# A fused two-layer transformer kernel: Strassen chunks with tiles of their own, a later start in their group, and y taken four tiles at a time

## The chip, the cores and the metric

One core of a Trainium2 chip runs the whole model in one launch. The metric is the device time of one execution in microseconds. The kernel before was run three times: 2220.4, 2224.18 and 2230.65 us, median 2224.18 us.

## What is computed

Two layers on 256 tokens of width 2048 in float32: stick-breaking attention with an MLP, then a sparse attention with three branches and an MLP. The change is in the two MLPs (layer 0 and layer 1):

```python
D_MODEL, SEQ, D_FF = 2048, 256, 4 * 2048

def sqrelu_mlp(h, w1, w2):
    return jnp.square(jax.nn.relu(h @ w1)) @ w2

for layer in range(2):
    h = h + (stick_breaking_attention, native_sparse_attention)[layer](rms_norm(h, ...), ...)
    h = h + sqrelu_mlp(rms_norm(h, mlp_norm_g[layer]), mlp_w1[layer], mlp_w2[layer])
```

## The kernel before, in words

**Products.** A float32 matrix is split in two parts, a rounded one (hi) and the rest (lo); of a product, hi times hi, lo times hi and hi times lo are summed in PSUM. The activations are split once. The weights come from HBM in chunks of 128x1024 float32 (512 KB, two slices of 128 rows by 512 columns), one DMA each on SP's queue (`load`, L130). For each chunk ScalarE (ACT) writes hi (L125), VectorE (DVE) writes lo as the difference (L127), then TensorE (PE) reads both. The raw chunks have five slots (`wraw`), the hi parts four (`whi`), the lo parts four (`wlo`). So a load can be issued only when the chunk five loads before it has been read to the end, which is when DVE has written its lo part.

**An MLP** (`mlp`, L418) goes through four groups `fg` of 2048 hidden columns. `group1` makes y = relu(x w1)^2 for the group: four blocks `fb` of four PSUM banks, eight chunks each (`proj_T2`, L186). After each block, two tiles of 128x256 at a time, ACT and DVE take y out of PSUM (L433 to L454): adds, relu and row factor, square, split in yhi and ylo, and four sums `q` that are split into `ss` for the Strassen block.

`group2` multiplies y with w2: four output blocks `nb` of 512 columns, eight chunks (k) each. Blocks 0, 1 and 3 are plain: `chunk_N` (L143), 12 matmuls of 512 columns. Block 2 takes one level of a Strassen-like scheme: `chunk_S` (L234) does seven half-size products in place of eight, 21 matmuls of 256 columns, and needs sums of the weight quarters. For such a chunk DVE makes four sums `ts` (L243, L247, L248), ACT writes the hi part of the plain quarters (L246, 768 columns) and of the sums (L125), DVE the lo part of the sums (L127) and of the plain quarters (L250). Both pairs come from the same four hi and four lo slots. PE takes first the 14 products with hi weights, then the 7 with lo weights.

**Order of the work.** `order` in `group2` (L459 to L465) lists the chunks as PE takes them and as SP loads them. Below, N0 to N23 are the plain chunks in that order (block 0, then 1, then 3) and S0 to S7 the Strassen ones. In the first three groups of a layer it is N0 N1 S0 N2 N3 S1 and so on to S7, then N16 to N23; in the last group S0 S1 N0 N1 S2 N2 N3 N4 N5 S3 and on by two. The order on DVE and ACT is set by a scheduler when the program is built; each of these engines then takes its instructions strictly as listed.

Of the kernel before, what the change touches and what calls it, by code (L numbers as in the profile page):

```python
# [8 lines left out]
F32 = mybir.dt.float32  # L9
# [30 lines left out]
def hybrid_kernel(  # L40
# [193 lines left out]
    def chunk_S(ps, src, k0, n0, first, last, ahi, alo, shi, slo, koff=0):  # L234


        W = NB // 2
        raw = load(src, k0, KC, n0, NB)
        flat = raw.rearrange("p k n -> p (k n)")

        ts = wsum.tile([P, 4, W], F32, tag="ts", name="ts")
        b12 = flat[:, 3 * W:].unsqueeze(1).to_broadcast([P, 2, W])
        nc.vector.tensor_tensor(ts[:, :2, :], flat[:, W:3 * W].rearrange("p (a n) -> p a n", a=2), b12, op=OP.subtract)  # L243
        hi = whi.tile([P, KC, NB], F32R, tag="hi", name="hi").rearrange("p k n -> p (k n)")
        lo = wlo.tile([P, KC, NB], F32R, tag="lo", name="lo").rearrange("p k n -> p (k n)")
        nc.scalar.activation(hi[:, :3 * W], flat[:, :3 * W], AF.Copy)  # L246
        nc.vector.tensor_tensor(ts[:, 2, :], ts[:, 0, :], flat[:, 2 * W:3 * W], op=OP.add)  # L247
        nc.vector.tensor_tensor(ts[:, 3, :], flat[:, :W], ts[:, 2, :], op=OP.subtract)  # L248
        thi, tlo = split(ts)
        nc.vector.tensor_tensor(lo[:, :3 * W], flat[:, :3 * W], hi[:, :3 * W].bitcast(F32), op=OP.subtract)  # L250
        k = k0 - koff
        y = lambda a, kk, t: a[:, k + kk, t * P:(t + 1) * P]
        s = lambda a, i: a[:, k // KC, i, :]
        b = lambda w, i: w[:, i * W:(i + 1) * W]
        trivial = [
            (0, y(ahi, 1, 0), y(alo, 1, 0), b(hi, 2), b(lo, 2)),
            (1, y(ahi, 0, 0), y(alo, 0, 0), b(hi, 0), b(lo, 0)),
            (2, s(shi, 3), s(slo, 3), b(hi, 1), b(lo, 1)),
        ]
        sums = [  # L260
            (6, s(shi, 2), s(slo, 2), thi[:, 0, :], tlo[:, 0, :]),
            (4, s(shi, 0), s(slo, 0), thi[:, 1, :], tlo[:, 1, :]),
            (5, s(shi, 1), s(slo, 1), thi[:, 2, :], tlo[:, 2, :]),
            (3, y(ahi, 0, 1), y(alo, 0, 1), thi[:, 3, :], tlo[:, 3, :]),
        ]

        def mm(i, a, w, s, e):
            nc.tensor.matmul(ps[i], a, w, start=s, stop=e, skip_group_check=True)  # L268

        for i, xh, xl, wh, wl in trivial + sums:  # L270

# [14 lines left out]
    def add_S(nb, bs, ps, pool):  # L286

        W = NB // 2
        u = pool.tile([P, 2, W], F32, tag="part", name="u")
        v = pool.tile([P, 2, W], F32, tag="pre", name="v")  # L290
        hb = [h[:, t, nb * NB:(nb + 1) * NB] for t in range(NT)]
        nc.scalar.activation(u[:, 0, :], ps[0], AF.Copy)
        nc.vector.tensor_tensor(v[:, 0, :], ps[5], u[:, 0, :], op=OP.add)
# [29 lines left out]
            )  # L323


    def make_x(kp, g0):

        ps = bank(att, "att")
        for j in range(2):
            for t in range(NT):  # L330
                nc.tensor.transpose(  # L331
# [24 lines left out]
    def next_x(layer, nb, g0):  # L356

        ssq(layer, nb, D // NB)
        for kp in range(nb * (NB // P), (nb + 1) * (NB // P), 2):
            yield  # L360
            make_x(kp, g0)

    def rsqrt(v, n):
        r = small.tile([P, 8], F32, tag="rsq", name="rsq", bufs=4)
# [53 lines left out]
    def mlp(l, layer, junk, done, last=None):  # L418
# [9 lines left out]
        def group1(fg, pools):  # L428

            for fb in range(D // NB):  # L430
                ps = [bank(*pools[fb % 2]) for _ in range(NB // P)]
                proj_T2(ps, w1, fg * D + fb * NB)
                for b in range(2):  # L433
                    k = fb * (NB // P) + 2 * b
                    c = junk.tile([P, 2, T], F32, tag="part", name="part")
                    a = junk.tile([P, 2, T], F32, tag="pre", name="pre")
                    for j in range(2):
                        nc.scalar.activation(c[:, j, :], ps[2 * b + j][:, T:], AF.Copy)
                        nc.vector.tensor_tensor(a[:, j, :], ps[2 * b + j][:, :T], c[:, j, :], op=OP.add)
                    nc.vector.scalar_tensor_tensor(  # L440
                        a, a, 0.0, row.unsqueeze(1).to_broadcast([P, 2, T]), op0=OP.max, op1=OP.mult
                    )
                    s = junk.tile([P, 2, T], F32, tag="sq", name="sq")
                    nc.scalar.activation(s, a, AF.Square)
                    nc.scalar.activation(yhi[:, k:k + 2, :], s, AF.Copy)
                    nc.vector.tensor_tensor(ylo[:, k:k + 2, :], s, yhi[:, k:k + 2, :].bitcast(F32), op=OP.subtract)

                    a1, a2 = [[s[:, kk, t * P:(t + 1) * P] for kk in (1, 0)] for t in range(NT)]
                    q = junk.tile([P, 4, P], F32, tag="sums", name="sums")
                    nc.vector.scalar_tensor_tensor(q[:, 0, :], a2[0], -1.0, a2[1], op0=OP.mult, op1=OP.subtract)  # L450
                    nc.vector.tensor_tensor(q[:, 2, :], a1[0], a2[0], op=OP.subtract)
                    nc.vector.tensor_tensor(q[:, 1, :], a2[1], q[:, 2, :], op=OP.subtract)
                    nc.vector.tensor_tensor(q[:, 3, :], a1[1], q[:, 1, :], op=OP.subtract)
                    split_evac(ss[:, 0, k // 2], ss[:, 1, k // 2], q)  # L454

        def group2(fg, plain, strassen, end):

            NK = KD // KC
            order = []  # L459
            for i in range(NK):  # L460
                pq = [(j // NK, j % NK) for j in (2 * i, 2 * i + 1)]
                order += [(2, i)] + pq if end else pq + [(2, i)]
            if end:
                order.insert(1, order.pop(3))
            order += [(3, i) for i in range(NK)]  # L465
            for nb, i in order:
                k0 = fg * KD + i * KC
                args = (w2, k0, nb * NB, i == 0, i == NK - 1, yhi, ylo)
                if nb == 2:
# [14 lines left out]
                if i == NK - 1:
# [2 lines left out]
                        return  # L487
                    add_h(nb, ps)
                    if end and nb == 3:
                        done(nb)  # L490
# [206 lines left out]

    with tc.tile_pool(name="m0p", bufs=2) as mp:
        wsum = mp
        def done0(nb):  # L700
            spawn(next_x("nsa", nb, G_NSA), 1.5)

        mlp(0, "m0", mp, done0)

# [352 lines left out]
    with tc.tile_pool(name="m1p", bufs=2) as mp:  # L1057
        wsum = mp
        ov = out[0].rearrange("(t p) d -> p t d", p=P)

        def done1(nb):
# [33 lines left out]
```

## Time and profile before

| what | value |
|---|---|
| median of three runs | 2224.18 us |
| the profiled execution | 2223.57 us, span 2221.8 us |
| PE busy, share of the span | 99% |
| DVE busy | 1542.2 us, 69% |
| ACT busy | 1226.2 us, 55% |
| mean granted TensorE clock | 0.998 |
| HBM traffic | 182 GB/s over the span |

Engines: PE is the matmul engine, PEld its weight loads, DVE VectorE, ACT ScalarE, SP the queue that issues the loads. Matmuls are pipelined: the duration shown for one is longer than the distance to the next, so a busy PE share of 99% does not exclude waits; they show in the length of a stretch.

### The profile page before, as it was taken

The page shows a single profiled execution, that of the slowest core. Times are in us where ns is not written, and L with a number is a line of the kernel's source. Part 1 is how long each engine was busy: PE and PEld are TensorE (multiplying, and loading weights), DVE is VectorE, ACT ScalarE, POOL GpSimd, SP SyncE. Part 2 cuts the span into 40 slices and gives each one's busy share as a digit, 9 for nine tenths or more (in the row PEclk, how much of TensorE's full clock was granted, in tenths as well). Part 3 has the DMA queues.
Part 4 walks back from the last instruction along what each step waited for, and adds up shares of the span by engine and source line. Part 5 has one row for each costly group of instructions (what it writes and reads, how often), then busy time and mean ns, then how long its engine had stood idle before and what let it go on. Part 6 is the DMA issues. An engine that isn't in the chain of part 4 may idle for free.

```text
span 2221.8 us, 31529 instructions
## 1 busy us (share of the span) xinstructions
PE 2197.6 (99%) x11922; PEld 1880.5 (85%) x11922; DVE 1542.2 (69%) x2320; ACT 1226.2 (55%) x1793; POOL 43.4 (2%) x75
## 2 busy tenths in 40 slices
PE   9999999999999999999999999999999999999999
PEld 9888888888888888888887888888888888888887
DVE  4656655677677677668777777756876776776785
ACT  5555665564455465455555666655644544554553
POOL 0000000000000000000000011000000000000000
PEclk9999999999999999999999999999999999999999
DMA  6655555656665665665667544456566557656655
GB/s 225 205 169 171 166 170 179 187 170 189 211 189 168 213 190 171 208 190 170 211 185 215 158 145 141 135 164 187 172 197 202 171 173 224 182 169 210 190 172 169
DMA packets 260769, 405.99 MB, mean 183 GB/s; under 512 B 13188, under 2 KB 91912, under 8 KB 260616
## 3 DMA queue, kind: packets, MB, share of 16 engines
q1 hardware_dynamic: 259800, 403.52, 58.2%
q8 instruction: 93, 1.52, 0.3%
q14 instruction: 60, 0.49, 0.1%
q10 hardware_dynamic: 816, 0.46, 0.1%
HBM read 401.83 MB, written 2.10 MB: 182 GB/s over the span
## 4 chain that ended last, share of the span: by engine, by line
PE 91%; DMA 4%; DVE 4%; issue 1%; ACT 0%; POOL 0%; DVEq 0%; ACTq 0%; SPq 0%; POOLq 0%
PE acc L147 33%; PE acc L193 11%; PE att L193 11%; PE att L147 6%; PE acc L213 5%; PE att L199 5%; PE acc L199 5%; DMA raw<-in_mlp_w_dram 4%; PE att L268 4%; PE acc L219 3%; DVE lo L127 2%; PE acc L176 2%; PE acc L268 1%; DVE lo L250 1%; PE att L331 1%
## 5 line engine op out<-in xcount | busy, mean ns | idle before, releaser
L125 ACT ACTIVATE hi<-raw 128x1024 fp32r<-128x1024 f32 x687 | 726.5, 1060 | 717.9 <-PE acc L147 268.0
L127 DVE TENSOR_TENSOR lo<-raw,hi 128x1024 fp32r<-128x1024 f32 x687 | 834.7, 1223 | 401.1 <-ACT hi L125 379.8
L147 PE MATMUL acc<-hi,yhi 128*128 128x512 f32 x828 | 327.0, 395 | 0.0
L147 PE MATMUL acc<-hi,ylo 128*128 128x512 f32 x828 | 325.0, 393 | 0.0
L193 PE MATMUL acc<-xs,hi 128*128 128x512 f32 x1024 | 259.8, 396 | 0.0
L193 PE MATMUL att<-xs,hi 128*128 128x512 f32 x1024 | 259.1, 395 | 0.0
L147 PE MATMUL acc<-lo,yhi 128*128 128x512 f32 x828 | 225.3, 393 | 1.1 <-DVE lo L127 1.1
L193 PEld LDWEIGHTS acc<-xs,hi 128*128 128x128 f32 x1024 | 183.0, 188 | 34.7 <-DVE h L387 0.3
L193 PEld LDWEIGHTS att<-xs,hi 128*128 128x128 f32 x1024 | 183.2, 188 | 34.5
L147 PEld LDWEIGHTS acc<-lo,yhi 128*128 128x128 f32 x828 | 154.8, 188 | 35.6 <-DVE lo L127 1.9
L147 PEld LDWEIGHTS acc<-hi,yhi 128*128 128x128 f32 x828 | 155.9, 188 | 31.7 <-ACT yhi L317 0.2
L147 PEld LDWEIGHTS acc<-hi,ylo 128*128 128x128 f32 x828 | 156.0, 188 | 31.3 <-DVE ylo L318 0.2
L147 PE MATMUL acc<-hi,xs 128*128 128x512 f32 x704 | 178.4, 394 | 0.0
L147 PEld LDWEIGHTS acc<-hi,xs 128*128 128x128 f32 x704 | 130.4, 188 | 27.4
L199 PEld LDWEIGHTS acc<-xs,lo 128*128 128x128 f32 x1024 | 135.9, 188 | 11.6
L199 PEld LDWEIGHTS att<-xs,lo 128*128 128x128 f32 x1024 | 135.9, 188 | 11.6
L199 PE MATMUL acc<-xs,lo 128*128 128x256 f32 x1024 | 137.6, 277 | 0.0
L199 PE MATMUL att<-xs,lo 128*128 128x256 f32 x1024 | 137.5, 277 | 0.0
L213 PE MATMUL acc<-xs,hi 128*128 128x512 f32 x512 | 130.3, 396 | 0.0
L243 DVE TENSOR_TENSOR ts<-raw 128x512 f32<-128x512 f32 x64 | 44.2, 691 | 103.8 <-DMA raw<-in_mlp_w_dram 103.8
L213 PEld LDWEIGHTS acc<-xs,hi 128*128 128x128 f32 x512 | 91.8, 188 | 17.5
L125 ACT ACTIVATE hi<-ts 128x1024 fp32r<-128x1024 f32 x64 | 67.6, 1056 | 65.1 <-DVE ts L248 46.7
(281 smaller groups left out, 2862.1 us busy)
## 6 DMA issues: line engine op xcount, KB each, us to landing
raw<-in_mlp_w_dram SPq DMA_DIRECT2D x512, 512.0 KB, 3.9
raw<-in_sb_w_qkv_dram SPq DMA_DIRECT2D x95, 512.0 KB, 3.9
raw<-in_nsa_w_in_dram SPq DMA_DIRECT2D x50, 512.0 KB, 3.6
raw<-in_sb_w_out_dram SPq DMA_DIRECT2D x32, 512.0 KB, 3.7
raw<-in_nsa_w_in_dram SPq DMA_DIRECT2D x64, 256.0 KB, 3.3
raw<-in_nsa_w_out_dram SPq DMA_DIRECT2D x32, 512.0 KB, 3.8
w1t<-in_nsa_cmp_w_dram SPq DMA_DIRECT2D x8, 512.0 KB, 4.4
h<-in_x_dram SPq DMA_DIRECT2D x8, 256.0 KB, 4.1
```

The source lines that it names most:

```text
L125: nc.scalar.activation(hi, raw, AF.Copy)
L127: nc.vector.tensor_tensor(lo, raw, hi.bitcast(F32), op=OP.subtract)
L147: mm = lambda a, b, k, t, s, e: nc.tensor.matmul(ps[t], a[:, k, t * P:(t + 1) * P], b, start=s, stop=e)
L176: nc.tensor.matmul(o, w[:, kk, m * P:(m + 1) * P], x[:, k0 + kk, :], start=s, stop=e, skip_group_check=True)
L193: nc.tensor.matmul(ps[m], hi[:, kk, m * P:(m + 1) * P], xs[:, k0 + kk, :, :].rearrange("p a t -> p (a t)"), start=k0 + kk == 0, stop=k0 + ...
L199: nc.tensor.matmul(ps[m][:, :T], lo[:, kk, m * P:(m + 1) * P], xhi[:, k0 + kk, :], start=False, stop=k0 + kk == KD - 1, skip_group_check=True,
L213: nc.tensor.matmul(ps[m], hi[:, kk, m * P:(m + 1) * P], xs[:, k0 + kk, :, :].rearrange("p a t -> p (a t)"), start=k0 + kk == 0, stop=k0 + ...
L219: nc.tensor.matmul(ps[m][:, :T], lo[:, kk, m * P:(m + 1) * P], xhi[:, k0 + kk, :], start=False, stop=k0 + kk == KD - 1, skip_group_check=True,
L243: nc.vector.tensor_tensor(ts[:, :2, :], flat[:, W:3 * W].rearrange("p (a n) -> p a n", a=2), b12, op=OP.subtract)
L250: nc.vector.tensor_tensor(lo[:, :3 * W], flat[:, :3 * W], hi[:, :3 * W].bitcast(F32), op=OP.subtract)
L268: nc.tensor.matmul(ps[i], a, w, start=s, stop=e, skip_group_check=True)
L331: nc.tensor.transpose(ps[:, j * T + t * P:j * T + (t + 1) * P], h[:, t, (kp + j) * P:(kp + j + 1) * P], ident)
```

## The change

Five edits, all in the MLP.

1. `chunk_S`: the hi and lo parts of the plain quarters get tiles of their own, `shi` and `slo`, one copy each (bufs=1), instead of taking a slot of `whi` and `wlo`. The lo part is written down ahead of the split of the sums, and in the pass with lo weights the plain quarters come first.
2. `group2`: a new rule for the order. In the first three groups of a layer: N0 to N4, S0, N5 N6 N7, S1, N8 N9, S2, N10 N11, S3, N12 N13, S4, N14 N15 N16, S5, N17 N18, S6, N19 N20, S7, N21 N22 N23. In the last: N0 to N3, S0, N4 N5, S1, N6 N7, S2, N8 N9, S3, N10, S4, N11 N12, S5, N13 N14, S6, N15 N16, S7, N17 to N23.
3. `group1`: y is taken out of PSUM four tiles at a time instead of two, with one copy of `pre`, `sq` and `sums`.
4. In the last group the plain blocks use the `att` banks and the Strassen block the `acc` banks (before: the other way round). `done` for blocks 0 to 2 is called after the last Strassen chunk, and layer 0's next x is made in the banks that this block has left.
5. `add_S` has its own tiles `u` and `v`.

```diff
 # chunk_S
-        hi = whi.tile([P, KC, NB], F32R, tag="hi", name="hi").rearrange("p k n -> p (k n)")
-        lo = wlo.tile([P, KC, NB], F32R, tag="lo", name="lo").rearrange("p k n -> p (k n)")
-        nc.scalar.activation(hi[:, :3 * W], flat[:, :3 * W], AF.Copy)
+        hi = wsum.tile([P, 3 * W], F32R, tag="shi", name="shi", bufs=1)
+        lo = wsum.tile([P, 3 * W], F32R, tag="slo", name="slo", bufs=1)
+        nc.scalar.activation(hi, flat[:, :3 * W], AF.Copy)
...
+        nc.vector.tensor_tensor(lo, flat[:, :3 * W], hi.bitcast(F32), op=OP.subtract)
         thi, tlo = split(ts)
-        nc.vector.tensor_tensor(lo[:, :3 * W], flat[:, :3 * W], hi[:, :3 * W].bitcast(F32), op=OP.subtract)
...
-        for i, xh, xl, wh, wl in sums + trivial:
+        for i, xh, xl, wh, wl in trivial + sums:
             mm(i, xh, wl, False, last)
 # group1
-                for b in range(2):
-                    k = fb * (NB // P) + 2 * b
-                    c = junk.tile([P, 2, T], F32, tag="part", name="part")
-                    a = junk.tile([P, 2, T], F32, tag="pre", name="pre")
...
+                k, n = fb * (NB // P), NB // P
+                a = junk.tile([P, n, T], F32, tag="pre", name="pre", bufs=1)
+                for j in range(n):
+                    c = junk.tile([P, T], F32, tag="part", name="part")
+                    nc.scalar.activation(c, ps[j][:, T:], AF.Copy)
+                    nc.vector.tensor_tensor(a[:, j, :], ps[j][:, :T], c, op=OP.add)
...
+                s = junk.tile([P, n, T], F32, tag="sq", name="sq", bufs=1)
...
+                q = junk.tile([P, 2, 4, P], F32, tag="sums", name="sums", bufs=1)
 # group2
-            order = []
-            for i in range(NK):
-                pq = [(j // NK, j % NK) for j in (2 * i, 2 * i + 1)]
-                order += [(2, i)] + pq if end else pq + [(2, i)]
-            if end:
-                order.insert(1, order.pop(3))
-            order += [(3, i) for i in range(NK)]
+            order, si = [], 0
+            for i in range(3 * NK):
+                order.append(((0, 1, 3)[i // NK], i % NK))
+                if si < NK and i >= (3 + 1.75 * si if end else 4 + 2.25 * si):
+                    order.append((2, si))
+                    si += 1
...
+                        if end:
+                            for n in range(3):
+                                done(n, strassen)
...
-            group2(fg, *((A, B) if end or fg % 2 == 0 else (B, A)), end)
+            group2(fg, *((A, B), (B, A))[fg % 2], end)
```

The scheduled order on DVE, before, in the second group of layer 0, from the lo parts of N10 and N11 to the sums of S7. `ts` are the sums of a Strassen chunk (`ts_6502` of S5, `ts_6573` of S6, `ts_6646` of S7); `lo<-ts` is the lo part of the sums, `lo<-raw` of 128x768 (L250) that of the plain quarters, `lo<-raw` of 128x1024 that of a plain chunk:

```order
L127 TENSOR_TENSOR lo_6468<-raw_6464,hi_6466 128x1024
L127 TENSOR_TENSOR lo_6486<-raw_6482,hi_6484 128x1024
L243 TENSOR_TENSOR ts_6573<-raw_6571 128x512
L127 TENSOR_TENSOR lo_6511<-ts_6502,hi_6509 128x1024
L250 TENSOR_TENSOR lo_6505<-raw_6500,hi_6504 128x768
L247 TENSOR_TENSOR ts_6573<-ts_6573,raw_6571 128x256
L248 TENSOR_TENSOR ts_6573<-raw_6571,ts_6573 128x256
L127 TENSOR_TENSOR lo_6539<-raw_6535,hi_6537 128x1024
L127 TENSOR_TENSOR lo_6557<-raw_6553,hi_6555 128x1024
L243 TENSOR_TENSOR ts_6646<-raw_6644 128x512
```

Before, the first sum of a Strassen chunk (S6) stands ahead of both lo parts of the chunk before it (S5), and behind the lo part of N10, whose raw slot S6's load takes.

The change, same engine and group, from the lo part of S3's sums to that of N14 (`ts_6344` is S3, `ts_6415` S4, `ts_6508` S5; `slo`, now L249, is the lo part of the plain quarters; the four plain chunks are N12, N13 and, last, N14):

```order
L127 TENSOR_TENSOR lo_6354<-ts_6344,hi_6352 128x1024
L243 TENSOR_TENSOR ts_6415<-raw_6413 128x512
L247 TENSOR_TENSOR ts_6415<-ts_6415,raw_6413 128x256
L249 TENSOR_TENSOR slo_6347<-raw_6342,shi_6346 128x768
L127 TENSOR_TENSOR lo_6381<-raw_6377,hi_6379 128x1024
L248 TENSOR_TENSOR ts_6415<-raw_6413,ts_6415 128x256
L127 TENSOR_TENSOR lo_6399<-raw_6395,hi_6397 128x1024
L127 TENSOR_TENSOR lo_6425<-ts_6415,hi_6423 128x1024
L243 TENSOR_TENSOR ts_6508<-raw_6506 128x512
L249 TENSOR_TENSOR slo_6418<-raw_6413,shi_6417 128x768
L127 TENSOR_TENSOR lo_6452<-raw_6448,hi_6450 128x1024
```

Now the lo part of the sums stands ahead of the next chunk's first sum, and the lo part of the plain quarters still behind it.

The change, DVE in the last group of layer 0, from the lo part of S3's sums to S4's `slo` (`ts_9424` is S3, `ts_9477` S4, `ts_9548` S5; the plain chunks are N10 and N11):

```order
L127 TENSOR_TENSOR lo_9434<-ts_9424,hi_9432 128x1024
L249 TENSOR_TENSOR slo_9427<-raw_9422,shi_9426 128x768
L127 TENSOR_TENSOR lo_9461<-raw_9457,hi_9459 128x1024
L127 TENSOR_TENSOR lo_9487<-ts_9477,hi_9485 128x1024
L243 TENSOR_TENSOR ts_9548<-raw_9546 128x512
L247 TENSOR_TENSOR ts_9548<-ts_9548,raw_9546 128x256
L248 TENSOR_TENSOR ts_9548<-raw_9546,ts_9548 128x256
L127 TENSOR_TENSOR lo_9514<-raw_9510,hi_9512 128x1024
L249 TENSOR_TENSOR slo_9480<-raw_9475,shi_9479 128x768
```

Here S4's `slo` stands behind all three sums of S5, and S5's load takes the raw slot of S3.

## Rows read from the trace of the kernel before

**Rows 1.** The page: busy time, share of the span and instructions of each engine.
```profile
PE 2197.6 (99%) x11922; PEld 1880.5 (85%) x11922; DVE 1542.2 (69%) x2320; ACT 1226.2 (55%) x1793; POOL 43.4 (2%) x75
```

**Rows 2.** Windows: group2 stretches, one group1 (second row). Length, busy PE, PEld, DVE, ACT, POOL, clock.
```profile
489.55:577.47 87.92, 86.48 (x458) 74.14 (x457) 66.23 (x89) 45.38 (x52) 0.00 (x0) 1.00 0.60 192
577.47:666.23 88.76, 88.76 (x513) 77.29 (x512) 61.14 (x93) 47.71 (x63) 0.00 (x0) 1.00 0.63 190
666.23:755.31 89.08, 86.91 (x459) 74.23 (x457) 66.11 (x89) 45.19 (x52) 0.00 (x0) 1.00 0.59 189
844.06:933.15 89.09, 86.91 (x459) 74.21 (x457) 66.15 (x89) 45.16 (x52) 0.00 (x0) 1.00 0.58 189
1021.90:1112.09 90.19, 89.37 (x482) 76.38 (x481) 72.06 (x104) 53.42 (x76) 3.37 (x12) 1.00 0.61 195
1594.37:1682.61 88.24, 86.65 (x459) 74.19 (x458) 66.11 (x89) 45.30 (x52) 0.00 (x0) 1.00 0.59 191
1771.36:1861.33 89.97, 86.91 (x459) 74.19 (x458) 66.20 (x89) 45.16 (x52) 0.00 (x0) 1.00 0.58 188
1950.08:2040.93 90.85, 88.49 (x458) 75.37 (x457) 66.76 (x90) 45.06 (x52) 0.00 (x0) 0.98 0.59 187
2129.69:2217.60 87.91, 86.72 (x464) 74.25 (x462) 64.05 (x87) 41.14 (x48) 0.00 (x0) 1.00 0.55 174
```

**Rows 3.** The chain that ended last: start us, us, what (xcount matmuls).
```profile
671.89 2.46 PE acc L268 x21
...
733.50 21.97 PE att L147 x96
```

**Rows 4.** Timeline of PE at one set of four transposes for layer 1's x.
```profile
1106.15 0.60 PE L331 MATMUL att<-ident,h 128*128 128x128 f32 x4
1106.51 0.48 PE L147 MATMUL acc<-hi,yhi 128*128 128x512 f32 x1
```

**Rows 5.** Windows: one plain chunk in the stretch from 1950.08 (columns as in rows 2).
```profile
2009.39:2013.73 4.34, 4.34 (x15) 3.43 (x13) 4.34 (x5) 2.52 (x3) 0.00 (x0) 0.61 0.68 206
```

**Rows 6.** Timeline of DVE, second group of layer 0: start, us, [idle before <-releaser].
```profile
675.94 0.69 DVE L446 TENSOR_TENSOR ylo<-sq,yhi 128x512 fp32r<-128x512 f32 x1
...
698.46 1.28 DVE L387 TENSOR_TENSOR h<-att,h 128x512 f32<-128x512 f32 x2
...
705.85 2.36 DVE L127 TENSOR_TENSOR lo<-raw,hi 128x1024 fp32r<-128x1024 f32 x2
712.51 0.69 DVE L243 TENSOR_TENSOR ts<-raw 128x512 f32<-128x512 f32 x1 [4.31 <-DMA raw<-in_mlp_w_dram]
713.12 1.22 DVE L127 TENSOR_TENSOR lo<-ts,hi 128x1024 fp32r<-128x1024 f32 x1
714.26 0.95 DVE L250 TENSOR_TENSOR lo<-raw,hi 128x768 fp32r<-128x768 f32 x1
715.13 0.42 DVE L247 TENSOR_TENSOR ts<-ts,raw 128x256 f32<-128x256 f32 x1
715.58 0.42 DVE L248 TENSOR_TENSOR ts<-raw,ts 128x256 f32<-128x256 f32 x1
715.92 2.35 DVE L127 TENSOR_TENSOR lo<-raw,hi 128x1024 fp32r<-128x1024 f32 x2
```

**Rows 7.** Timeline of PE in the same place: S5's first matmuls with lo weights.
```profile
714.40 0.63 PE L268 MATMUL acc<-lo,ss 128*128 128x256 f32 x3 [0.94 <-DVE lo L127]
```

**Rows 8.** The chain that ended last, same place: loads of S5 and S6.
```profile
697.77 4.64 DMA raw<-in_mlp_w_dram
...
707.09 5.40 DMA raw<-in_mlp_w_dram
```

**Rows 9.** DMA issues, KB each, median us to landing: whole kernel, then 666 to 745 us.
```profile
raw<-in_mlp_w_dram SPq DMA_DIRECT2D x512, 512.0 KB, 3.9
...
raw<-in_mlp_w_dram SPq DMA_DIRECT2D x29, 512.0 KB, 4.9
```

More of the change, by code (lines that the diff above doesn't have):

```diff
@@ L288, in add_S @@
         W = NB // 2
-        u = pool.tile([P, 2, W], F32, tag="part", name="u")
-        v = pool.tile([P, 2, W], F32, tag="pre", name="v")
+        u = pool.tile([P, 2, W], F32, tag="u", name="u", bufs=1)
+        v = pool.tile([P, 2, W], F32, tag="v", name="v", bufs=1)
         hb = [h[:, t, nb * NB:(nb + 1) * NB] for t in range(NT)]
@@ L323, in split_evac, with make_x @@
             )
-    def make_x(kp, g0):
-        ps = bank(att, "att")
+    def make_x(kp, g0, pool=None):
+        ps = bank(*pool or (att, "att"))
         for j in range(2):
@@ L354, in ssq, with next_x @@
             )
-    def next_x(layer, nb, g0):
+    def next_x(layer, nb, g0, pool=None):
         ssq(layer, nb, D // NB)
@@ L360, in next_x @@
             yield
-            make_x(kp, g0)
+            make_x(kp, g0, pool)
     def rsqrt(v, n):
@@ L432, in group1 @@
                 proj_T2(ps, w1, fg * D + fb * NB)
-                for b in range(2):
-                    k = fb * (NB // P) + 2 * b
-                    c = junk.tile([P, 2, T], F32, tag="part", name="part")
-                    a = junk.tile([P, 2, T], F32, tag="pre", name="pre")
[L437 to L454, printed above, removed]
@@ new lines, in group1 @@
+                k, n = fb * (NB // P), NB // P
[4 more added lines that the diff above has]
+                    nc.vector.tensor_tensor(a[:, j, :], ps[j][:, :T], c, op=OP.add)
+                nc.vector.scalar_tensor_tensor(
+                    a, a, 0.0, row.unsqueeze(1).to_broadcast([P, n, T]), op0=OP.max, op1=OP.mult
+                )
@@ new lines, in group1 @@
+                s = junk.tile([P, n, T], F32, tag="sq", name="sq", bufs=1)
+                nc.scalar.activation(s, a, AF.Square)
+                nc.scalar.activation(yhi[:, k:k + n, :], s, AF.Copy)
+                nc.vector.tensor_tensor(ylo[:, k:k + n, :], s, yhi[:, k:k + n, :].bitcast(F32), op=OP.subtract)
+                sv = s.rearrange("p (j kk) t -> p j kk t", kk=2)
+                a1, a2 = [[sv[:, :, kk, t * P:(t + 1) * P] for kk in (1, 0)] for t in range(NT)]
+                q = junk.tile([P, 2, 4, P], F32, tag="sums", name="sums", bufs=1)
@@ L456, in group2 @@
+                nc.vector.scalar_tensor_tensor(q[:, :, 0, :], a2[0], -1.0, a2[1], op0=OP.mult, op1=OP.subtract)
+                nc.vector.tensor_tensor(q[:, :, 2, :], a1[0], a2[0], op=OP.subtract)
+                nc.vector.tensor_tensor(q[:, :, 1, :], a2[1], q[:, :, 2, :], op=OP.subtract)
+                nc.vector.tensor_tensor(q[:, :, 3, :], a1[1], q[:, :, 1, :], op=OP.subtract)
+                split_evac(ss[:, 0, k // 2:k // 2 + 2], ss[:, 1, k // 2:k // 2 + 2], q)
         def group2(fg, plain, strassen, end):
@@ L477, in group2 @@
                     ps = [bank(*plain) for _ in range(NT)]
-                    if end and nb == 3:
-                        for n in range(3):
-                            done(n)
                 out = last is not None and end and nb == 3
@@ L489, in group2 @@
                     if end and nb == 3:
-                        done(nb)
+                        done(nb, plain)
         spawn(rows(), 1)
@@ L699, in hybrid_kernel, with done0 @@
         wsum = mp
-        def done0(nb):
-            spawn(next_x("nsa", nb, G_NSA), 1.5)
+        def done0(nb, pool):
+            spawn(next_x("nsa", nb, G_NSA, pool), 1.5)
         mlp(0, "m0", mp, done0)
@@ L1059, in hybrid_kernel, with done1 @@
         ov = out[0].rearrange("(t p) d -> p t d", p=P)
-        def done1(nb):
+        def done1(nb, pool):
             if nb < D // NB - 1:
```

## The prediction

> **What bounds the kernel now.** I read the busy table first, then the length of each stretch against the work in it, then the chain of waits and the timelines where a stretch is longer than its work. PE is busy 99% of the span [rows 1], so only a wait of PE can be won back. A plain chunk takes PE 21.97 / 8 = 2.75 us (96 matmuls are eight chunks) and a Strassen chunk 2.46 us [rows 3]. A group2 stretch therefore has 24 x 2.746 + 8 x 2.46 = 85.59 us of work. The eight stretches are 713.25 us long together [rows 2], 28.5 us more than 8 x 85.59. Of this, six sets of transposes for layer 1 at 0.36 us take 2.2 us of the fourth stretch [rows 4]. 26.4 us of lost time are left, 1.2% of the run, and that is the ceiling. The two stretches of the last groups (1021.90 and 2129.69) lose 2.4 and 2.3 us, the six others 21.6 us. One plain chunk took 4.34 us at a granted clock that fell from 2.4 to 1.2 GHz for part of it (mean 0.61) [rows 5], which is 1.6 us of the 21.6. The six lose 20.0 us by waits, 3.3 us each. A group1 stretch has PE busy for all of its 88.76 us [rows 2], so nothing can be won there.
>
> **Where the waits come from.** The timeline of DVE shows a loop [rows 6]. The lo part of N10 starts at 705.85. When it is done its raw slot is free, and the load of S6 (five loads on) starts at 707.09 and takes 5.40 us [rows 8]. DVE stands still for 4.31 us at S6's first sum, with both lo parts of S5 queued behind it. Then come that sum (0.61 us to the next start), S5's lo of the sums (1.14), its lo of the quarters (0.87), two more sums (0.45, 0.34), and at 715.92 the lo part of N12, whose end starts the next such load. The loop is 10.07 us; PE needs 2 x 2.746 + 2.46 = 7.95 us for the two plain chunks and one Strassen chunk in it. PE shows it as a wait of 0.94 us at S5's lo weights [rows 7].
>
> So the price of the loop is the load. I take 5.0 us for it, the mean of 4.64 and 5.40 [rows 8], beside 4.9 us, the median in this stretch; over the kernel it is 3.9 us [rows 9]. In the page DMA: Bandwidth & Descriptors (section Anatomy of one DMA — SWDGE (gpsimd) path) the Trainium skill gives a load 2.0 us plus its bytes over 436 GB/s, fitted for another issue path; that would be 3.2 us here, an estimate, and by it the sum would come out as in the first rival. The row of 5.40 us speaks against it, so the sum goes by the rows.
>
> **The change, part by part.**
>
> *The order on DVE, first three groups of a layer.* I add up each loop from the start of one plain chunk's lo part to that of the next whose raw slot matters: 1.24 us to the issue, 5.0 of load, 0.02, then what stands behind the wait. What stands inside the 5.0 us costs nothing. Before, from N4: 8.88, 6.87, 9.67, 9.67, 9.67 us for N4 to N6, to N8, N10, N12 and N14, against 7.95 each, together 5.0 us too long. PE loses 3.3, so DVE starts with a lead of 1.7 us. After, by the new order: N8 to N10 10.16 (two adds to h, 1.28 us [rows 6], and both lo parts of S2 stand behind S3's wait), N10 to N12 8.19 (S3's lo of the sums now lies inside the load of S4), N12 to N13 1.48 against 2.75, N13 to N15 9.67, N15 to N17 7.66, N17 to N19 9.67. Together that is 4.3 us too long. The lead is what I cannot read: S0 starts after five plain chunks and not two (13.7 and not 5.5 us into the group), which gives DVE time, but it runs ahead only as far as four hi, four lo and five raw slots let it. Its ends are 1.7 us as before (PE loses 2.6) and 4.3 us (PE loses nothing). I take 2.3, nearer the measured end, so 2.0 us lost per group. **Gain: 6 x (3.3 - 2.0) = 8.0 us.**
>
> *Own tiles.* They make the reordering possible: a Strassen chunk takes one hi and one lo slot and not two. `slo` has one copy, written again only when PE has read it, 2 us into the Strassen chunk before; the next one needs it 3.7 to 6 us later and DVE needs 0.95 us for it, so this costs nothing by itself. What is late next is `slo`: it still stands behind the next Strassen chunk's first sum (S4's behind S5's, S6's behind S7's), and since the plain quarters now open the pass with lo weights, PE will wait for `slo` where it waited for the lo part of the sums.
>
> *The last group of a layer.* Only N10 lies between S3 and S4 there. S4's `slo` stands behind S5's sums, and S5's load behind S3's `slo`: 5.02 + 0.61 + 0.45 + 0.34 + 1.14 (N11's lo) + 0.95 = 8.5 us from one `slo` to the next, against 2.46 + 2.75 = 5.2 us on PE. S4 is late by 3.3 us less the lead of S3's `slo`; ends 0 and 3.3. I take 2.9, because the lead there is small by the same loops. Before, these stretches lose 2.4 us. **Loss: 2 x 0.5 = 1.0 us.**
>
> *y four at a time.* Per block DVE runs three 1024-wide instructions instead of six 512-wide ones (1.14 for 2 x 0.60 us by the starts in [rows 6]) and four sums instead of eight: under 1 us less, in group1, where PE waits for nothing [rows 2]. Cost and gain nothing. The last block's y comes later: its `ylo` was written 9.7 us into the group (675.94 against 666.23) [rows 2, 6]. Twice the width on ACT and DVE adds some 3 us. Its first reader, N6, now starts 6 x 2.746 + 2.46 = 18.9 us into the group. Were this cover gone, N6 would wait for what is missing, once per group.
>
> *Banks, `done`, `u` and `v`.* The same matmuls, transposes and adds go to other banks; the three outputs are issued among the last seven chunks as before, and SP's loads keep their order. Nothing on the path, either way.
>
> *Clock.* One 1.2 GHz stretch costs 1.6 us now [rows 5]. It came behind waits of the same kind. I keep one; none would give 1.6 us, two more would cost 3.2.
>
> **Sum:** 8.0 - 1.0 = 7.0 us. The profiled execution took 2223.57 us, 0.6 below the median, so 2216.6 by it and **2217 us** by the median: 0.3% less. I call a difference over 0.5% (11 us, 2213 or 2235) faster or slower, which is about what a measurement of this kernel tells from none.
>
> **Rivals.**
>
> *The loads get short.* If the wider spacing takes the loads out of each other's way, they come in 3.9 us [rows 9]. Each loop is then 1.1 us shorter, the sum of all falls below PE's, and no group of the first kind waits; the last groups lose 1.8 us each. 2223.6 - 20.0 - 1.6 - (4.8 - 3.6) = 2201 us. For it: 3.9 us is the median of 512 loads. Against: DVE still frees raw slots in bursts after each wait (N10's lo, N11's lo, S5's `slo` about 1 us apart before; S3's `slo`, N12, N13 after), and the load in such a burst is the 5.40 us one. Chance 0.30. The Trainium skill's estimate above (DMA: Bandwidth & Descriptors, Anatomy of one DMA — SWDGE (gpsimd) path) would end at this rival.
>
> *`slo` becomes the bound.* With `slo` last in line and one copy of it, every 0.1 us on the load costs 0.1 us in five loops of six groups. At 5.6 us the loops are 7.3 too long, 5.0 us lost per group of the first kind, 3.5 in the last ones: 30 + 7 = 37 us of waits, two more 1.2 GHz stretches 3.2, against 24.8 of waits now: 2223.6 + 15.4 = 2239 us. It breaks even at 5.3 us and is slower by over 0.5% from 5.6 us. For it: 5.40 us is a measured load, and after the change the load that decides (S5) is issued third in its burst. Against: the median is 4.9 us. In Trainium Kernel Development and Optimization, section Best Practices, the Trainium skill asks for two buffers where transfers and work are to overlap, and one copy of `slo` goes against that. Chance 0.10.
>
> *Nothing moves.* The new lead is used up at the start of a group and the loops, 4.3 us too long where they were 5.0, lose as much as before: 2221 to 2224 us. Chance 0.13.
>
> **How the numbers follow.** The forecast's own range is 2209 to 2222 us, chance 0.47, of which 0.03 falls below 2213. Faster: 0.30 + 0.03 = 0.33. Slower: 0.10. Within 0.5%: 0.57. The range from 2202 to 2231 leaves out the low end of the first rival and the second one, under 2 in 10.
>
> **What would show it.** Right: the six stretches are 87 to 88.5 us long; PE's waits in them stand before `slo` (L249), at S4 and S6; the two last groups are 88 to 89 us long, with one wait of 2 to 3 us before S4's lo weights; DVE still waits over 10 us per group at L243; group1 stays at 88.8 us. Wrong: no waits at L243 over 3 us and stretches near 85.7 (first rival); waits at three or more Strassen chunks of a group, loads over 5.4 us (second); a wait before N6 or in group1 would mean that y's cover failed.

## The result, and the profile after

The changed kernel took **2202.36 us** (median of four runs, 2201.79 to 2203.22), the kernel before 2224.05 us beside it: the ratio is 0.990, 95% interval 0.9876 to 0.9923. The forecast was 2217 us: the sign was right and the size three times too small. The profiled execution took 2201.79 us, 21.8 less than the one of before.

The page and the waits of PE (us in total, times, longest), changed kernel. PE is busy as before [rows 1], the median load is 4.2 us and not 3.9 [rows 9], and of the waits of PE in the MLPs one kind is left, three times (2.6 and 0.4 us in the last group of layer 1, 0.3 us in the stretch from 1755.61):

```profile
PE 2187.0 (99%) x11922; PEld 1875.4 (85%) x11922; DVE 1537.9 (70%) x2096; ACT 1204.4 (55%) x1697; POOL 42.6 (2%) x75
...
raw<-in_mlp_w_dram SPq DMA_DIRECT2D x512, 512.0 KB, 4.2
...
PE acc L268 <- DVE slo L249: 3.4, 3, 2.6
```

Windows of the changed kernel, the eight group2 stretches in order and one group1 (second row); columns as in [rows 2] (the last two are the busy share of the DMA engines and GB/s):

```profile
487.43:573.03 85.60, 85.60 (x459) 73.77 (x458) 67.08 (x86) 44.04 (x48) 0.00 (x0) 1.00 0.61 194
573.03:661.78 88.75, 88.75 (x514) 77.32 (x512) 59.53 (x69) 46.96 (x55) 0.00 (x0) 1.00 0.65 192
661.78:747.38 85.60, 85.60 (x459) 73.77 (x457) 67.29 (x86) 43.17 (x48) 0.00 (x0) 1.00 0.62 194
836.13:921.73 85.60, 85.60 (x458) 73.77 (x457) 67.27 (x86) 43.12 (x48) 0.00 (x0) 1.00 0.61 195
1010.48:1098.95 88.47, 88.47 (x483) 76.28 (x482) 71.11 (x99) 51.31 (x72) 2.54 (x12) 1.00 0.63 196
1581.26:1666.86 85.60, 85.60 (x459) 73.77 (x457) 66.93 (x86) 44.12 (x48) 0.00 (x0) 1.00 0.61 194
1755.61:1841.88 86.27, 85.94 (x458) 73.90 (x457) 67.23 (x86) 42.98 (x48) 0.00 (x0) 1.00 0.61 192
1930.64:2016.26 85.62, 85.62 (x459) 73.79 (x458) 67.11 (x86) 42.98 (x48) 0.00 (x0) 1.00 0.60 193
...
2104.99:2195.85 90.86, 87.83 (x464) 75.35 (x462) 63.14 (x82) 38.63 (x44) 0.00 (x0) 0.98 0.51 166
```

A group2 stretch has 85.59 us of work. Five of the six stretches of the first three groups are now that long to within 0.03 us, the sixth (1755.61) 0.7 us more: together 514.29 us against 535.15 before [rows 2], **20.9 us less**. The last group of layer 0 is 1.7 us shorter (88.47 for 90.19), that of layer 1 2.9 us longer (90.86 for 87.91). A further 2.1 us lie ahead of the first MLP, where the change edits nothing: the first stretch starts at 487.43 and not 489.55. Of this, 0.8 us are there already near the start of the run, where PE goes on behind a wait of 1.9 us at 14.71 and not 15.52. The rest goes with the clock: in the profile of before it fell to 1.2 GHz for 3.4 us at 16.5 us, 1 us behind that wait, and here, behind the same wait, it did not. Sum: 20.9 + 1.7 - 2.9 + 2.1 = 21.8 us.

What did not go away is DVE's wait for loads at L243. In the second group of layer 0, first before, then after the change:

```profile
DVE ts L243 <- DMA raw<-in_mlp_w_dram: 13.3, 5, 4.3
```
```profile
DVE ts L243 <- DMA raw<-in_mlp_w_dram: 14.3, 6, 4.2
```

DVE stands still for a load as long as it did, and PE no longer notices.

### The profile page after: what moved, and what is told of

It is laid out like the page before. It is cut to its first block, busy times and chain, and to the rows that moved or that the text cites. A ratio compares the mean times of both kernels' runs of the same rounds, so it can differ in the third digit from the quotient of the medians.

```text
span 2200.1 us, 31289 instructions
## 1 busy us (share of the span) xinstructions
PE 2187.0 (99%) x11922; PEld 1875.4 (85%) x11922; DVE 1537.9 (70%) x2096; ACT 1204.4 (55%) x1697; POOL 42.6 (2%) x75
## 4 chain that ended last, share of the span: by engine, by line
PE 98%; DVE 1%; DMA 0%; POOL 0%; ACT 0%; issue 0%; DVEq 0%; ACTq 0%; POOLq 0%
PE acc L147 31%; PE att L147 13%; PE acc L193 11%; PE att L193 11%; PE acc L213 5%; PE acc L199 5%; PE att L199 5%; PE att L268 4%; PE acc L268 3%; PE acc L219 3%; PE acc L176 2%; PE att L926 1%; PE att L331 1%; PE att L918 0%; DMA raw<-in_mlp_w_dram 0%; PE att L919 0%
## 5 line engine op out<-in xcount | busy, mean ns | idle before, releaser
L193 PE MATMUL acc<-xs,hi 128*128 128x512 f32 x1024 | 259.8, 396 | 0.0
L147 PE MATMUL acc<-hi,yhi 128*128 128x512 f32 x640 | 251.7, 394 | 0.0
L147 PE MATMUL acc<-hi,ylo 128*128 128x512 f32 x640 | 250.6, 392 | 0.0
L193 PEld LDWEIGHTS acc<-xs,hi 128*128 128x128 f32 x1024 | 183.0, 188 | 34.7 <-DVE h L387 0.3
L147 PE MATMUL acc<-lo,yhi 128*128 128x512 f32 x640 | 174.1, 393 | 0.0
L147 PE MATMUL att<-hi,ylo 128*128 128x512 f32 x380 | 149.7, 394 | 0.0
L147 PE MATMUL att<-hi,yhi 128*128 128x512 f32 x380 | 149.4, 393 | 0.0
L147 PEld LDWEIGHTS acc<-lo,yhi 128*128 128x128 f32 x640 | 119.6, 188 | 25.8 <-issue 0.4
L147 PEld LDWEIGHTS acc<-hi,ylo 128*128 128x128 f32 x640 | 120.3, 188 | 24.5 <-DVE ylo L318 0.2
L147 PEld LDWEIGHTS acc<-hi,yhi 128*128 128x128 f32 x640 | 120.2, 188 | 24.3 <-ACT yhi L317 0.2
L243 DVE TENSOR_TENSOR ts<-raw 128x512 f32<-128x512 f32 x64 | 44.3, 692 | 128.9 <-DMA raw<-in_mlp_w_dram 128.9
```

The costliest lines, as they stand in the source:

```text
L147: mm = lambda a, b, k, t, s, e: nc.tensor.matmul(ps[t], a[:, k, t * P:(t + 1) * P], b, start=s, stop=e)
L193: nc.tensor.matmul(ps[m], hi[:, kk, m * P:(m + 1) * P], xs[:, k0 + kk, :, :].rearrange("p a t -> p (a t)"), start=k0 + kk == 0, stop=k0 + ...
```

## Experiments

All times are medians; each ratio is against the kernel before on the same chip, with its 95% interval. Four hypotheses run through them. **L**: the later S0 gives DVE its head start. **T**: the own tiles do it. **R**: what counts is what stands in a loop on DVE around the wait for a load. **H** and **S**: the number of hi and lo slots, or of raw slots, decides how far DVE can run ahead. Further letters (N, O, Y) are explained in the expectation that uses them.

### Which edit it was

Own tiles alone (edit 1 of the five; the chunk order, banks and y as before). Edit 1 has three parts: the tiles, the lo part of the plain quarters written ahead of the split of the sums, and the plain quarters first in PE's pass with lo weights. No run takes them apart, so which of them changes the order on DVE is not shown; "own tiles" below stands for all three.

```diff
-        hi = whi.tile([P, KC, NB], F32R, tag="hi", name="hi").rearrange("p k n -> p (k n)")
-        lo = wlo.tile([P, KC, NB], F32R, tag="lo", name="lo").rearrange("p k n -> p (k n)")
+        hi = wsum.tile([P, 3 * W], F32R, tag="shi", name="shi", bufs=1)
+        lo = wsum.tile([P, 3 * W], F32R, tag="slo", name="slo", bufs=1)
...
-        for i, xh, xl, wh, wl in sums + trivial:
+        for i, xh, xl, wh, wl in trivial + sums:
```

> The kernel before with edit 1 alone: shi and slo are tiles of their own, and the plain quarters open the pass with lo weights; the order of chunks, the banks and y are as before. Theory L (the lead: what was won is DVE's head start, and it comes from S0 standing after five plain chunks): S0 still stands after two here, so PE's waits stay, 2215 to 2224 us. Theory T (the own tiles: the scheduler can now put the lo part of the sums ahead of the next chunk's first sum, inside its load, so that 1.24 + 5.0 + 0.02 + 0.61 + 0.45 + 0.87 = 8.2 us stand in a loop where 9.67 stood, against 7.95 of PE): the waits of the six first groups go almost wholly, 2203 to 2209 us.

Measured: **2197.23 us, ratio 0.9873 (0.9859 to 0.9888)**. It beats the whole change by 5 us, and falls below the span that theory T gave, since the last groups gain too (88.5 and 85.8 us, before 90.2 and 87.9). In the second group of layer 0 the stretch has no loss, and DVE's waits at L243 are 53.2 us over the whole run, where before there were 103.8 and after the change 128.9. On DVE the lo part of S5's sums (699.64) stands ahead of S6's first sum (702.18), which waits for its load; that of S5's plain quarters (703.25) still stands behind it:

```profile
661.76:747.37 85.61, 85.61 (x459) 73.77 (x458) 66.20 (x90) 43.67 (x51) 0.00 (x0) 1.00 0.62 194
...
DVE ts L243 <- DMA raw<-in_mlp_w_dram: 53.2, 37, 3.3
...
699.64 1.23 DVE L127 TENSOR_TENSOR lo<-ts,hi 128x1024 fp32r<-128x1024 f32 x1
702.18 0.69 DVE L243 TENSOR_TENSOR ts<-raw 128x512 f32<-128x512 f32 x1 [1.32 <-DMA raw<-in_mlp_w_dram]
...
703.25 0.95 DVE L249 TENSOR_TENSOR slo<-raw,shi 128x768 fp32r<-128x768 f32 x1
```

The new order alone (edit 2, `done` called after the last Strassen chunk), y four at a time alone (edit 3, with `u` and `v`), and the change without its own tiles (edits 2 to 5):

```diff
 # the new order alone, against the kernel before
-                order += [(2, i)] + pq if end else pq + [(2, i)]
...
+                if si < NK and i >= (3 + 1.75 * si if end else 4 + 2.25 * si):
+                    order.append((2, si))
+                    si += 1
 # y four at a time alone, against the kernel before
-                for b in range(2):
...
+                k, n = fb * (NB // P), NB // P
+                a = junk.tile([P, n, T], F32, tag="pre", name="pre", bufs=1)
 # no own tiles, against the changed kernel
-        hi = wsum.tile([P, 3 * W], F32R, tag="shi", name="shi", bufs=1)
-        lo = wsum.tile([P, 3 * W], F32R, tag="slo", name="slo", bufs=1)
+        hi = whi.tile([P, KC, NB], F32R, tag="hi", name="hi").rearrange("p k n -> p (k n)")
+        lo = wlo.tile([P, KC, NB], F32R, tag="lo", name="lo").rearrange("p k n -> p (k n)")
```

> The kernel before with the new order of chunks alone (done is called after the last Strassen chunk; hi and lo of the plain quarters still take slots of whi and wlo; y two at a time). Theory L (lead by the later start): the gain is all or nearly all here, 2202 to 2208 us. Theory T (own tiles): the loops between two plain chunks are still 9.67 us long because both lo parts of a Strassen chunk stand behind the next one's first sum, so PE waits 1.5 to 3 us per group of the first kind, and the last groups as before: 2212 to 2220 us.

> The kernel before with y taken four tiles at a time and u, v as tiles of add_S, nothing else. Theories L and T: no loop and no lead hangs on it, 2219 to 2227 us, waits of PE before lo of the sums as before. Rival Y (DVE's backlog at the start of a group is what it starts behind with; fewer and wider instructions cut it): 2208 to 2217 us.

> The changed kernel without the own tiles: shi and slo take slots of whi and wlo again, with the old order inside the chunk; the new order of chunks, y four at a time, banks, u and v stay. Theory T (own tiles): the loops are 9.6 us long as in the run of the new order alone, so PE waits: 2208 to 2222 us. Rival O (the new order and y together give DVE a lead that lasts for the group): 2205 us or less.

Measured: order alone 2217.71 us, 0.9966 (0.9954 to 0.9978), inside theory T's span; y alone 2217.73 us, 0.9963 (0.9948 to 0.9978), between what the two sides expected; both and the banks without own tiles **2224.80 us, 0.9996 (0.9983 to 1.0009)**, even above theory T's span. Each is worth 0.3% by itself and together they are worth nothing; why the two small gains do not add is not settled. In the profile of the order alone PE waits 1.8 us at the first plain chunk of each last group, and the clock falls to 1.2 GHz for 3.4 us behind it: the plain blocks still take the banks there that the last block of y has just left. With the banks of edit 4 this wait does not appear. The waits of the kernel without own tiles, of PE and of DVE, are of the kind of before again:

```profile
PE acc L268 <- DVE lo L127: 4.2, 5, 1.0
PE att L268 <- DVE lo L127: 3.9, 7, 0.8
...
DVE ts L243 <- DMA raw<-in_mlp_w_dram: 153.1, 60, 4.6
```

The changed kernel with y two at a time, as it was before, and `u` and `v` in the tiles that they had before:

```diff
-                a = junk.tile([P, n, T], F32, tag="pre", name="pre", bufs=1)
...
+                for b in range(2):
+                    c = junk.tile([P, 2, T], F32, tag="part", name="part")
+                    a = junk.tile([P, 2, T], F32, tag="pre", name="pre")
```

> The changed kernel with y taken two tiles at a time as before (and the part and pre tiles for the Strassen adds). Theories L and T: 2200 to 2206 us, as with four. Rival Y: part of the waits come back, 2208 us or more.

Measured: 2197.36 us, 0.9876 (0.9861 to 0.9891), a little below the span. So the gain is the own tiles' alone; of the other edits y four at a time, with `u` and `v`, costs 5 us here.

### Why the own tiles do it

The kernel before, with raw slots of their own for the Strassen chunks and everything else left:

```diff
-    def load(src, k0, nk, n0, nn):
-        raw = wraw.tile([P, nk, nn], F32, tag="raw", name="raw")
+    def load(src, k0, nk, n0, nn, own=None):
+        if own:
+            raw = own[0].tile([P, nk, nn], F32, tag=own[1], name=own[1], bufs=own[2])
+        else:
+            raw = wraw.tile([P, nk, nn], F32, tag="raw", name="raw")
...
-        raw = load(src, k0, KC, n0, NB)
+        raw = load(src, k0, KC, n0, NB, (wsum, "sraw", 2))
```

> The kernel before, in which the raw chunks of the Strassen block get two slots of their own (sraw) beside the five of wraw; hi and lo slots, order of the chunks and y as before, and on DVE both lo parts of a Strassen chunk still stand behind the next one's first sum. Theory R (a load stands inside DVE's loop, because a raw slot comes free so late): a Strassen chunk's load no longer waits for a plain chunk's lo part, the waits of DVE at its first sum go, and PE's with them: 2195 to 2201 us. Theory H (the own tiles win by giving hi and lo a fifth slot, which lets DVE run further ahead): hi and lo are as before, so PE waits as before, 2216 to 2226 us.

Measured: 2208.81 us, 0.9929 (0.9914 to 0.9944), between the two spans and in neither, but the stretches decide. All six of the first groups are 85.8 us long, though both lo parts of S4, S5 and S6 still stand behind the next chunk's first sum (L246 is what L243 was):

```profile
664.07:749.90 85.83, 85.83 (x458) 73.97 (x457) 69.67 (x95) 45.53 (x52) 0.00 (x0) 1.00 0.64 197
...
DVE ts L246 <- DMA sraw<-in_mlp_w_dram: 21.6, 19, 4.0
```

With the load out of the loop the loss is gone: theory R, where the loop was looked for. This kernel also has seven raw slots in all, so rival S stays open until the runs with four below. What the profiled execution, the slowest of the four (2211.88 us), still loses sits in the last groups: PE waits 4.3 us for lo parts of plain chunks, and the clock falls to 1.2 GHz for 3.4 us in one and 6.8 us in the other.

Own tiles with three hi and three lo slots, so that there are four of each as before; and the two kernels with four raw slots instead of five:

```diff
 # own tiles, three slots
-    whi = ctx.enter_context(tc.tile_pool(name="whi", bufs=4))
-    wlo = ctx.enter_context(tc.tile_pool(name="wlo", bufs=4))
+    whi = ctx.enter_context(tc.tile_pool(name="whi", bufs=3))
+    wlo = ctx.enter_context(tc.tile_pool(name="wlo", bufs=3))
 # four raw slots: in the kernel before, and in own tiles alone
-    wraw = ctx.enter_context(tc.tile_pool(name="wraw", bufs=5))
+    wraw = ctx.enter_context(tc.tile_pool(name="wraw", bufs=4))
```

> Own tiles alone, with whi and wlo cut from four slots to three, so that with shi and slo there are four hi and four lo parts as before. On DVE both lo parts of a Strassen chunk stand ahead of the next one's first sum. Theory R: the loop is 1.24 + 5.0 + 0.02 + 0.61 + 0.45 + 0.34 = 7.7 us, below PE's 7.95, so no waits come back: 2195 to 2203 us. Theory H: with the fifth part taken away the waits come back, 2212 to 2224 us.

> The kernel before with four raw slots (wraw) instead of five, nothing else. The scheduler then writes both lo parts of a Strassen chunk directly behind its own sums, ahead of the next one's first sum. Theory R (what counts is what stands behind a load's wait within one loop on DVE): from the lo part of N11 to that of N13 there are now 1.24 + 5.0 + 0.02 + 0.61 + 0.45 = 7.3 us, less than PE's 7.95, so this kernel is faster than the one before with a raw slot less: 2197 to 2210 us. Rival S (the number of slots decides how far DVE runs ahead): one slot less makes the waits longer, 2228 us or more.

> Own tiles alone with four raw slots instead of five. Theory R: the loops are 7.3 to 7.7 us, below PE's 7.95, so nothing is lost in the stretches: 2195 to 2203 us. Rival S (number of slots): waits come back, 2206 us or more.

Measured: three slots 2198.47 us, 0.9886 (0.9869 to 0.9902): the number of hi and lo parts is not it. Before with four raw slots **2208.89 us, 0.9931 (0.9915 to 0.9948): a slot less, and 15 us faster.** Own tiles with four raw slots 2199.83 us, 0.9890 (0.9876 to 0.9905). All three fell in theory R's spans. The stretch of before with four raw slots, its waits at L243 over the run (before: 103.8 us), and DVE from the lo part of N11 (second of the two at 703.33) to that of N13 (712.62):

```profile
664.31:751.34 87.03, 86.30 (x459) 74.09 (x457) 68.28 (x92) 44.93 (x52) 0.00 (x0) 1.00 0.62 194
...
DVE ts L243 <- DMA raw<-in_mlp_w_dram: 39.6, 18, 5.0
...
703.33 2.36 DVE L127 TENSOR_TENSOR lo<-raw,hi 128x1024 fp32r<-128x1024 f32 x2
...
708.41 1.23 DVE L127 TENSOR_TENSOR lo<-ts,hi 128x1024 fp32r<-128x1024 f32 x1 [1.21 <-ACT hi L125]
709.55 0.95 DVE L250 TENSOR_TENSOR lo<-raw,hi 128x768 fp32r<-128x768 f32 x1
710.42 1.22 DVE L127 TENSOR_TENSOR lo<-raw,hi 128x1024 fp32r<-128x1024 f32 x1
711.56 0.68 DVE L243 TENSOR_TENSOR ts<-raw 128x512 f32<-128x512 f32 x1
712.28 0.42 DVE L247 TENSOR_TENSOR ts<-ts,raw 128x256 f32<-128x256 f32 x1
712.62 1.22 DVE L127 TENSOR_TENSOR lo<-raw,hi 128x1024 fp32r<-128x1024 f32 x1
```

Both lo parts of S5 (708.41 and 709.55) stand ahead of S6's first sum, which no longer waits. Before, they stood behind it, after a wait of 4.31 us [rows 6]. From 704.47 to 712.62 it is 8.15 us, not the 7.3 expected, since DVE waits 1.21 us for ACT's hi part ahead of 708.41; before, from N10 to N12, it was 10.07 us. That is still a little over PE's 7.95 us, and the six stretches, 86.0 to 87.0 us long, still lose 0.4 to 1.4 us each.

### What the order is for

The changed kernel with y two at a time and S0 early; with the old order; and with two plain chunks between all Strassen chunks of the last groups:

```diff
 # S0 early (y two at a time)
-                if si < NK and i >= (3 + 1.75 * si if end else 4 + 2.25 * si):
+                if si < NK and i >= (3 + 1.75 * si if end else 1 + 2.25 * si):
 # old order, banks and done
-                if si < NK and i >= (3 + 1.75 * si if end else 4 + 2.25 * si):
...
+                order += [(2, i)] + pq if end else pq + [(2, i)]
 # last groups by twos
-                if si < NK and i >= (3 + 1.75 * si if end else 4 + 2.25 * si):
+                if si < NK and i >= (3 + 2 * si if end else 4 + 2.25 * si):
```

> The changed kernel with y two at a time, and S0 after two plain chunks instead of five in the first three groups of a layer, at the same spacing behind it. Theory L (the later start of S0 gives the lead that the loops use up): PE waits at two or more Strassen chunks of each group, 2203 to 2212 us. Theory T (the lead comes from the own tiles, wherever S0 stands): 2195 to 2200 us.

> The changed kernel with the order of the chunks, the banks and the calls of done as before: own tiles, u, v and y four at a time remain. Theory T (own tiles) with N: nothing is lost against own tiles alone, 2195 to 2199 us. Theory Y: the later y costs a wait in one group or more here too, 2200 to 2206 us. If the order were needed for the gain: 2210 us or more.

> The changed kernel with the rule of the last groups from 3 + 1.75 si to 3 + 2 si, so that two plain chunks stand between every two Strassen chunks (S3, N10, N11, S4) and S7 comes one plain chunk later. Theory N (the single plain chunk between S3 and S4 leaves slo too late): the wait of 2.6 us and the 1.2 GHz stretch behind it in the last group go, 2196 to 2199 us. Theory Y (y taken four at a time lets DVE start the group too late, wherever the chunks stand): the wait stays at some Strassen chunk of that group, 2200 to 2204 us.

Measured: S0 early **2196.82 us, 0.9876 (0.9862 to 0.9891)**: theory L falls, where S0 stands does not matter once the tiles are there. Old order with y four at a time 2207.44 us, 0.9920 (0.9905 to 0.9934), outside what the theories gave (between Y and a need for the order), by a wait that none had named:

```profile
PE att L268 <- DVE pre L438: 6.5, 5, 1.7
...
849.56 1.05 PE L268 MATMUL att<-hi,ss 128*128 128x256 f32 x4 [1.67 <-DVE pre L438]
```

S0 takes the banks that the last block of y has just left, and y four at a time leaves them too late when S0 comes after two plain chunks. With the own tiles in place, the later S0 of the change covers just that, and nothing else that these runs show.

Last groups by twos: 2198.28 us, 0.9880 (0.9865 to 0.9895). The last group of layer 1 is then 85.64 us long, where the change has 90.86:

```profile
2106.86:2192.50 85.64, 85.64 (x464) 73.97 (x462) 63.00 (x82) 38.67 (x44) 0.00 (x0) 1.00 0.54 176
```

So the 5 us by which the change misses own tiles alone sit there. They need the single plain chunk N10 and y four at a time together, since taking away either one ends them (with y two at a time and N10 single, that group is 85.62 us long).

Against 2202.36 us for the change, own tiles alone (2197.23), the change with y two at a time (2197.36) and that with S0 early (2196.82) are the fastest kernels here. They do not differ from each other measurably, and no PE wait is left in their group2 stretches.

## Why the prediction was right in sign and wrong in size

**What bounds the kernel: right.** The loss sat in the waits of the six first stretches, behind a load inside DVE's loop; taking that load out of the loop ended them.

**The loops after the change: right in sum.** Forecast from the start of N8's lo part to N19's: 46.83 us. The trace has 682.87 to 729.35, 46.48 us, 4.0 too long for PE's 42.5 (forecast 4.3).

**The failing step is the lead.** The prediction took 1.7 us before the change, as the difference of two sums (loops 5.0 us too long, PE loses 3.3), and from it 2.3 us after, with 4.3 as its end. The lead can be read: from the end of a lo part on DVE to PE's first matmul with it. Before the change for N4, where the loops begin (the first of the two lo parts at 679.55 takes 1.22 us and ends at 680.77; the last line is N14's):

```profile
679.55 2.36 DVE L127 TENSOR_TENSOR lo<-raw,hi 128x1024 fp32r<-128x1024 f32 x2
...
684.02 0.62 PE L147 MATMUL att<-lo,yhi 128*128 128x512 f32 x2
...
725.53 2.35 DVE L127 TENSOR_TENSOR lo<-raw,hi 128x1024 fp32r<-128x1024 f32 x2
```

That is 3.25 us, not 1.7. The sum that it was taken from was too small: N14's lo part starts at 725.53, so the five loops took 45.98 us and not 44.76, 6.2 us too long. Nor was the lead used up: PE, which lost 3.4 us on the way, reaches N14's lo part at 727.17, 0.4 us after it is done. After the change, N8, where the loops were counted from:

```profile
682.87 2.35 DVE L127 TENSOR_TENSOR lo<-raw,hi 128x1024 fp32r<-128x1024 f32 x2
...
690.50 0.39 PE L147 MATMUL att<-lo,yhi 128*128 128x512 f32 x1
```

The first of the two ends at 684.09: a lead of **6.4 us** where 2.3 was taken. Less the 4.0 us that the loops use up, 2.4 are left at N19 (729.35 + 1.22, PE at 733.01). In this group the lead never runs out, hence no wait, although the loops are too long. The smallest one is 0.94 us, at S6's `slo` (729.43, 730.37). Worth: the forecast's sum was -7.0 us, the two profiled executions differ by -21.8. Of the 14.8 us between them 12.9 lie in the six stretches: the 12.0 us of waits charged for too small a lead, and 1.6 us for the clock, less the 0.7 us of 1755.61. 2.1 us lie at the start, and the last groups came out 0.2 us dearer than said (+1.2 for +1.0). That these two agree is luck: each was to lose 0.5 us, and layer 0's gained 1.7 where layer 1's lost 2.9.

**Where the lead comes from.** It was put down to the later S0. But own tiles alone has 4.9 us at N4 with S0 after two plain chunks (lo part ready at 674.64, PE at 679.50), and the new order alone has 3.8 us at N8 with S0 after five (690.99, 694.77). The change without own tiles, which differs from it in edit 1 only, has 3.0 us at N8 (692.12, 695.16). In the order alone DVE still waits at S2's first sum with both lo parts of S1 queued behind it:

```profile
686.36 0.69 DVE L243 TENSOR_TENSOR ts<-raw 128x512 f32<-128x512 f32 x1 [3.03 <-DMA raw<-in_mlp_w_dram]
686.97 1.22 DVE L127 TENSOR_TENSOR lo<-ts,hi 128x1024 fp32r<-128x1024 f32 x1
688.11 0.95 DVE L250 TENSOR_TENSOR lo<-raw,hi 128x768 fp32r<-128x768 f32 x1
689.77 1.22 DVE L127 TENSOR_TENSOR lo<-raw,hi 128x1024 fp32r<-128x1024 f32 x1
```

So the prediction was right that the own tiles make the reordering possible, and wrong to price that reordering only in the loops from N8 on and to give the lead to the later S0: the own tiles move the lo part of the sums ahead of the wait from the first Strassen chunk on, also in the stretch before N8, which the loops were not counted for.

**The last groups: the mechanism right, in one of two.** Forecast: one wait before S4's lo weights, 2.9 us. In layer 1 it came, at S4, behind S5's three sums as said (the first fence is PE, the second DVE):

```profile
2150.20 0.51 PE L268 MATMUL acc<-slo,yhi 128*128 128x256 f32 x2 [2.62 <-DVE slo L249]
...
2152.19 0.63 PE L147 MATMUL att<-hi,ylo 128*128 128x512 f32 x1
2152.62 0.63 PE L147 MATMUL att<-hi,yhi 128*128 128x512 f32 x1
```
```profile
2146.53 0.69 DVE L243 TENSOR_TENSOR ts<-raw 128x512 f32<-128x512 f32 x1 [2.25 <-DMA raw<-in_mlp_w_dram]
...
2148.06 1.22 DVE L127 TENSOR_TENSOR lo<-raw,hi 128x1024 fp32r<-128x1024 f32 x1
2149.19 0.95 DVE L249 TENSOR_TENSOR slo<-raw,shi 128x768 fp32r<-128x768 f32 x1
```

In layer 0 the lead covered it. The one 1.2 GHz stretch that was kept stands behind that wait, not in a first group: N11's matmuls come 0.43 us apart (2152.19 and 2152.62) where 0.23 is usual.

**y four at a time: wrong.** It was said to cost nothing, with N6's cover as the risk, and it costs 5 us. The risk was at the banks, and at the start of the last group, where DVE stands 4.24 us at S1's first sum with two of the four adds of y behind it:

```profile
2111.57 0.69 DVE L243 TENSOR_TENSOR ts<-raw 128x512 f32<-128x512 f32 x1 [4.24 <-DMA raw<-in_mlp_w_dram]
```

That load was one of four issued within 4.2 us, and took 7.1 us. In the profile of the version by twos it is one of four issued within 4.3 us, takes 4.8 us, and DVE waits 1.90 us at the same place. So how much of the 5 us is y's, and how much the longer load's, stays open; the four runs of the change lie within 1.4 us of each other, so it is not a matter of this one execution.

**The rivals.** The first one gave 2201 us and its time came true, by another road: loads did not get short (4.2 us in the median, DVE's longest wait at L243 5.0). Of its signs, stretches near 85.7 us came, and the absence of waits over 3 us at L243 did not. `slo` as the bound did not appear, though one copy of it is all there is (by the prediction's own terms that rival breaks even at 5.2 us and not 5.3, which changes nothing here). The Trainium skill's price of a load (DMA: Bandwidth & Descriptors, section Anatomy of one DMA — SWDGE (gpsimd) path), fitted there for another issue path and an estimate of 3.2 us here, does not agree with the median of 4.2 us. The Trainium skill's rule of two buffers (Trainium Kernel Development and Optimization, section Best Practices) speaks of overlapping transfers with work; carried over to `slo`, which DVE writes, it is not borne out: with one copy, own tiles alone has no wait of PE in its group2 stretches, and DVE waits 2.4 us in the whole run for PE to be done with that copy. Of what was to show the forecast right, the waits at L243 over 10 us per group, group1 at 88.8 us and one of the two last groups (88.5 us) were so, and the lengths of the six stretches and of the other last group (90.9 us) were not.

## What to carry to other kernels

Where an in-order engine waits for a load, list what stands behind the waiting instruction and who needs it: work that is ready and stands behind that wait is lost time, and the same work ahead of it is free; here that made a kernel with one slot less faster. Read the lead directly, from the end of a producer to its consumer's first use, at the point where the loops begin; a lead that is the difference of two sums carries the errors of both. Run each edit alone: one of five edits gave all of the gain, and another gave part of it back.

## What was not expected

A raw slot less made the kernel before 15 us faster (2208.89 us), because the scheduler, which sets the order on DVE, then put the lo parts elsewhere: a change of a size is a change of order too, and has to be read on the queue.

The 1.2 GHz stretch of 3.4 us near the start appeared in eleven of the fourteen profiled executions and not in three (the change; own tiles alone; the change without own tiles), though in all fourteen PE waits 1.9 us just ahead of that place. In the profiles of before, of the new order alone and of own tiles with three slots, which have it, all that follows is 1.8 to 2.1 us later than in those of the change and of own tiles alone. The 1.2 GHz stretches further on in these profiles, too, stand behind waits of PE, of 1.5 to 2.6 us. Profiled executions are compared by their stretches for that reason.
